# A row maximum that skips NaNs: one load in one piece, no trial write-backs, and a bias given as a number

## The chip, the cores and the metric

The kernel runs on one core of a Trainium2 chip. The metric is device time in microseconds (us) of one execution, lower is better. Of the core's engines it uses ScalarE (ACT in the profile), POOL (GpSimd), VectorE (DVE) and SyncE (SP), which issues all transfers. TensorE has no work.

## What is computed

```python
batch, seq, dim = 32, 2048, 2048
x = np.random.randn(batch, seq, dim).astype(np.float32)
mask = np.random.rand(batch, seq, dim) < 0.1
x[mask] = np.nan
...
def reference(x, axis):        # axis = -1
    return np.nanmax(x, axis=axis).astype(np.float32)
```

The input is 65,536 rows of 2,048 f32 values, 536.87 MB; a tenth of the values are NaN. The output is the largest value of each row that is not NaN, 0.26 MB.

## The kernel before

**Tiles.** The rows are cut into 74 tiles, listed by hand in `TILES` (L16). A tile holds up to 7 rows for each of the 128 partitions, 14,336 columns of 4 bytes, and is counted in quarters of a row (`Q`, 512 columns). Each entry of `TILES` has three lists: how the tile is loaded, in how many pieces it is cleaned, and in how many it is reduced. Most tiles are `[28], [7, 9, 12], [16, 12]`: one load of 28 quarters (7,168 KB in all), three pieces of 7, 9 and 12 quarters, and two reductions of 16 and 12 quarters (4 rows and 3). The first tile is one row, and the last dozen tiles have ever smaller loads and pieces. Below, tiles are counted from 0; `number` in the code is one more.

**What is done with a tile.** A NaN would spoil a maximum, so it is replaced first, by way of the upper 16 bits of each value, read as int16 (every second int16 of the tile):

- ScalarE's *key pass* (L432) reads these halves with a stride of two and writes a dense uint16 key into one of three key buffers `kts`. It computes `Prelu(EDGE - half)`. Its slope `alpha` sends the halves of NaNs, which lie above `EDGE`, to keys that come back as very negative numbers. Its bias `EDGE` (32639.25) is read from memory: `top`, a column of the tile `scalars`, filled at L274.
- The *write-back* turns the key into a half again (`TOP - key`) and writes it into the tile, with a stride of two. POOL does it (L453), or ScalarE for the pieces with a negative sign in `TILES` (L407).
- VectorE's reduction (L478) takes the maximum of the whole f32 rows into `acc`.

At the end of groups of tiles, rows in which nothing was found are marked (`find`, L250) and results are stored (L511).

**What sets the order.** Each engine runs its instructions in the order of the program. `Order` (L119) adds the semaphore waits that data and buffers ask for. Three facts matter for the change:

- There are three tile buffers (`xts`, `BUFS`), so the load of tile n waits until the reductions of tile n - 3 are done (`free`, L346 and L490). SyncE issues loads in order, so a load that waits holds back all behind it.
- A key pass waits for its tile's load, and for a key buffer that the write-backs have left.
- Each load has one of 14 semaphores in turn (`LANES`, L331).

**The parts that the change touches.** `spare` (L280) is called once, after tile 0 (L491). It runs eighteen instructions on columns 2,048 and up of buffer 0, which tile 0 does not use: six on each of POOL, ScalarE and VectorE, in that order, each computing `1 - x` on 1,024 int16 values a partition, with dense, strided and blocked patterns of reading and writing. Their results are read by nothing. What they read is filled with zeros first (L277). The load of tile 3, the next in that buffer, waits for the last of each engine (L492). With `number == SPLIT` (L353) tile 29 is loaded by nine transfers in place of one: for each of four column ranges of 1,024 to 1,408 columns, one transfer for the first 8, 120, 64 or 16 partitions and one for the others (`BLOCKS`), and one for the remaining 9,472 columns.

Of the kernel before, what the change touches and what calls it, by code (L numbers as in the profile page):

```python
# [8 lines left out]
D = 2048  # L9
# [54 lines left out]

LANES = 14

LEFT = D
SOME = 1024
SPLIT = 30
BLOCKS = ((1024, 8), (1152, 120), (1280, 64), (1408, 16))  # L70

# [4 lines left out]
EDGE = TOP + 0.25  # L78
# [99 lines left out]
def kernel(  # L178
# [15 lines left out]
    nc = tc.nc  # L194
    P = nc.NUM_PARTITIONS
    f32, i32 = mybir.dt.float32, mybir.dt.int32
    i16, u16 = mybir.dt.int16, mybir.dt.uint16
    ALU = mybir.AluOpType
    ACT = mybir.ActivationFunctionType
# [7 lines left out]
    of = out.bitcast(i32).flatten_outer_dims().rearrange("r c -> (r c)")  # L207
# [16 lines left out]
    with tc.tile_critical():  # L224
        order = Order(nc)

        def act(deps, pair=None, **kw):
            return order.add(
                "act",
                nc.scalar,  # L230
                lambda: nc.scalar.activation(**kw),  # L231
                deps,
                lane=pair,
                joint=pair is not None,
            )
# [38 lines left out]
        e_top = order.add("dve", nc.vector, lambda: nc.vector.memset(top, EDGE), [])  # L274
        act([e_top], out=warm, in_=top, func=ACT.Prelu, alpha=0.5)

        zeros = xts[0][:, LEFT : LEFT + SOME // 2 + SOME]  # L277
        e_zero = order.add("dve", nc.vector, lambda: nc.vector.memset(zeros, 0), [])  # L278

        def spare(room):  # L280

            half = SOME // 2
            of = room[:, 0:half].bitcast(i16)
            apart = room[:, half : half + SOME].bitcast(i16)[:, 1::2]
            e = e_zero
            ends = []
            at = half + SOME

            def place():
                nonlocal at  # L290
                at += SOME
                return room[:, at - SOME : at].bitcast(i16)

            def turns(v, j):
                return v.rearrange("p (j i) -> p i j", j=j)

            for who, engine in (("pool", nc.gpsimd), ("act", nc.scalar), ("dve", nc.vector)):
                to = place()
                far, near = to[:, 1::2], to[:, 0:SOME]
                forms = [(far, of), (near, of), (near, apart), (far, apart)]  # L300
                forms += [(turns(far, j), turns(of, j)) for j in (2, 32)]
                d = [e]
                for o, i in forms:
                    if who == "act":
                        d = [act(d, out=o, in_=i, func=ACT.Copy, bias=1.0, scale=-1.0)]
                        continue
                    d = [
                        order.add(
                            who,
                            engine,  # L310
                            lambda: engine.tensor_scalar(  # L311
                                out=o, in0=i, scalar1=-1.0, scalar2=1.0, op0=ALU.mult, op1=ALU.add
                            ),
                            d,
                        )
                    ]
                ends += d
            return ends

        free = [[] for _ in range(BUFS)]  # L320
        kfree = [[] for _ in range(NKEYS)]
        clock = 0
# [14 lines left out]
        for gi, (s, g) in enumerate(zip(rows, GROUPS)):  # L337
# [6 lines left out]
            for loads, pieces, reds in g:  # L344
# [4 lines left out]
                at = 0  # L349
                for c in loads:  # L350
                    c *= Q
                    runs = [(at, at + c, 0, P)]
                    if number == SPLIT:  # L353
                        runs = []
                        a = at
                        for n, p in BLOCKS:
                            runs += [(a, a + n, 0, p), (a, a + n, p, P)]
                            a += n
                        runs += [(a, at + c, 0, P)]
                    for a, b, p, q in runs:  # L360
                        e = order.add(
                            "sp",
                            nc.sync,
                            lambda: nc.sync.dma_start(  # L364
                                out=xt[p:q, a:b], in_=xg[p:q, base + a : base + b]
                            ),
                            before + lanes[turn],
                            lane=f"load{turn}",
                            step=16,
                        )  # L370
                        lanes[turn] = [e]
                        turn = (turn + 1) % LANES
                        landed.append((a, b, e))
                    at += c
                clean = []
                after = []
# [42 lines left out]
                for parts in pieces:  # L419
                    parts = parts if isinstance(parts, tuple) else (parts,)  # L420
                    c = int(sum(map(abs, parts))) * Q
                    here = [l for a, b, l in landed if a < at + c and b > at]
                    kold = []
                    if used + c > KEYS:
                        key = (key + 1) % NKEYS
                        used = 0
                        kold, kfree[key] = last(kfree[key]), []
                        assert all(k != key for q in half.values() for _, _, k, _, _ in q)
                        if at + c == sum(loads) * Q:

                            kold = kold + last(kfree[(key + 1) % NKEYS])
                    e_key = act(  # L432
                        here + kold,
                        out=kts[key][:, used : used + c],
                        in_=xt[:, at : at + c].bitcast(i16)[:, 1::2],
                        func=ACT.Prelu,
                        bias=top,
                        scale=-1.0,
                        alpha=float(TOP - LOW) / (EDGE - NAN),
                    )  # L440
                    release()
                    for c in parts:
                        back, wait, c = c < 0, isinstance(c, float), int(abs(c)) * Q
                        kp = kts[key][:, used : used + c]
                        used += c
                        to = xt[:, at : at + c].bitcast(i16)[:, 1::2]
                        at += c
                        if back:
                            held.append((at - c, at, key, kp, e_key, piece))
                            if not wait or at == sum(loads) * Q:  # L450
                                release()
                        else:
                            e = pool(  # L453
                                [e_key],
                                name(piece),
                                out=to,
                                in0=kp,
                                scalar1=-1.0,
                                scalar2=float(TOP),
                                op0=ALU.mult,  # L460
                                op1=ALU.add,
                            )
                            cleaned(at - c, at, key, piece, e)
                        piece += 1
                        open_ = [h[0] for h in held] + [p[0] for q in half.values() for p in q]
                        while reds and done + reds[0] <= min([at] + open_):
                            n = reds.pop(0)


                            lo = done - 1 if done % D else done  # L470
                            done += n
                            row = (base + lo) // D
                            if done % D:
                                m, to = 1, xt[:, done - 1 : done].bitcast(f32)
                            else:
                                m = max(n // D, 1)
                                to = acc[:, row : row + m]
                            e = dve(  # L478
                                [e for a, b, e in clean if b > lo and a < done] + part,
                                nc.vector.tensor_reduce,  # L480
                                out=to,
                                in_=xt[:, lo:done]
                                .bitcast(f32)
                                .rearrange("p (c d) -> p c d", c=m),
                                axis=mybir.AxisListType.X,
                                op=ALU.max,
                            )
                            part = [e] if done % D else []
                            after.append(e)
                free[(number - 1) % BUFS] = after[-1:]  # L490
                if number == 1:  # L491
                    free[0] = free[0] + spare(xt[:, LEFT:])  # L492
                base += at
            stores.append((og, acc.bitcast(i32)))
            if gi == LATE:
# [61 lines left out]
```

## Time and profile before

| what | value |
| --- | --- |
| time, median of 3 runs (lowest to highest) | 1265.29 us (1263.24 to 1266.24) |
| span of the profiled execution | 1263.2 us |
| instructions in the profile | 926 |
| VectorE busy | 1134.3 us (90%), of it reductions 1109.3 |
| ScalarE busy | 1000.7 us (79%), of it key passes 935.1 (247) |
| POOL busy | 1188.0 us (94%), of it write-backs 1171.5 (236) |
| trial write-backs | VectorE 22.2, POOL 15.5, ScalarE 14.4 us (6 each) |
| transfers | 537.2 MB, 425 GB/s over the span |

The profiled execution is one of its own. Its time is the span, from the first instruction to the last; the lowest of the runs lies 0.04 us above it, the median 2.1 us.

In the profile's rows a line number such as L231 can be that of a helper: all ScalarE instructions carry L231, POOL's write-backs L241, VectorE's reductions L248, the trials of POOL and VectorE L311. They are told apart by what they read and write: `kt<-xt,scalars` is a key pass, `xt<-kt` a write-back, `xt<-xt` a trial, `acc<-xt` a reduction. Buffer numbers are left out. A row in order of time has start, length, engine, line, operation, shape of the first instruction merged into it, their count, and in brackets how long the engine had been idle and what ended that. A row of the list of groups has the count, total busy time and mean length in ns, then idle time. A row of the table of waits has the total in us, how often, and the longest. All loads together are the page's DMA row; an engine that moves a part of a transfer counts as busy while it has a packet in flight.

### The profile page before, as it was taken

What the parts mean: (1) busy time and instruction counts of PE and PEld (TensorE: products, weight loads), DVE (VectorE), ACT (ScalarE), POOL (GpSimd) and SP (SyncE); (2) the same over time, 40 slices, a digit from 0 to 9 for tenths busy, and PEclk for the clock granted to TensorE, in tenths of its full rate; (3) what the DMA queues carried; (4) which work ended last, traced back from release to release, by engine and by line L of the source; (5) the groups of instructions that cost most, each with busy time, mean ns of one, the idle gap of its engine ahead of it and who ended that gap; (6) DMA issues with size and microseconds to landing.
All of it is one profiled execution on the core that took longest, in us unless ns stands there. A gap on an engine that the chain in (4) does not pass through costs nothing.

```text
span 1263.2 us, 926 instructions
## 1 busy us (share of the span) xinstructions
DVE 1134.3 (90%) x188; ACT 1000.7 (79%) x279; POOL 1188.0 (94%) x248
## 2 busy tenths in 40 slices
DVE  7788988888889988788888889888888999999999
ACT  7767787778787876678777977777778778999998
POOL 7999989998999899798999899999999999989998
DMA  9999999999999999999999999999999999999997
GB/s 411 407 434 421 436 432 431 436 434 432 434 436 434 436 436 318 439 434 436 434 436 432 432 436 430 434 430 432 434 436 434 436 432 423 432 435 431 427 429 289
DMA packets 16613, 537.20 MB, mean 425 GB/s; under 512 B 2654, under 2 KB 2654, under 8 KB 4190
## 3 DMA queue, kind: packets, MB, share of 16 engines
q1 hardware_dynamic: 16606, 537.14, 99.3%
q14 instruction: 7, 0.06, 0.0%
HBM read 536.87 MB, written 0.26 MB: 425 GB/s over the span
## 4 chain that ended last, share of the span: by engine, by line
DMA 34%; DVE 26%; POOL 25%; ACT 14%; issue 1%; SPq 0%; ACTq 0%
DMA xt<-in_x_dram 34%; DVE acc L248 26%; POOL xt L241 23%; ACT kt L231 13%; ACT xt L231 2%; POOL xt L311 1%; SPq L364 0%; DVE none L254 0%; DVE acc L268 0%; SPq L552 0%; ACTq L163 0%; SPq L224 0%
## 5 line engine op out<-in xcount | busy, mean ns | idle before, releaser
L241 POOL TENSOR_SCALAR xt<-kt 128x3584 int16<-128x3584 uint16 (+11 forms) x236 | 1171.5, 4964 | 69.8 <-ACT kt L231 51.9
L248 DVE TENSOR_REDUCE acc<-xt 128x3 f32<-128x6144 f32 (+4 forms) x175 | 1107.6, 6379 | 124.6 <-POOL xt L241 116.7
L231 ACT ACTIVATE kt<-xt,scalars 128x3584 uint16<-128x3584 int16 (+9 forms) x247 | 935.1, 3825 | 255.2 <-DMA xt<-in_x_dram 223.4
L231 ACT ACTIVATE xt<-kt 128x512 int16<-128x512 uint16 (+6 forms) x24 | 52.8, 2202 | 0.7
L311 DVE TENSOR_SCALAR xt<-xt 128x1024 int16<-128x1024 int16 x6 | 22.2, 3702 | 0.2
L311 POOL TENSOR_SCALAR xt<-xt 128x1024 int16<-128x1024 int16 x6 | 15.5, 2576 | 0.5
L231 ACT ACTIVATE xt<-xt 128x1024 int16<-128x1024 int16 x6 | 14.4, 2402 | 0.2
L231 ACT ACT_TABLE_LOAD x1 | 1.3, 1283 | 0.9 <-SPq L224 0.9
L248 DVE TENSOR_REDUCE xt<-xt 128x1 f32<-128x1536 f32 x1 | 1.7, 1745 | 0.0
L278 DVE MEMSET xt<- 128x1536 int32 x1 | 1.3, 1338 | 0.3 <-issue 0.3
L274 DVE MEMSET scalars<- 128x1 f32 x1 | 0.1, 59 | 1.0 <-SPq L224 1.0
L254 DVE TENSOR_SCALAR none<-acc 128x414 int32<-128x414 f32 (+1 forms) x2 | 0.8, 381 | 0.1
L268 DVE TENSOR_TENSOR acc<-acc,none 128x414 int32<-128x414 int32 (+1 forms) x2 | 0.7, 374 | 0.1
L254 POOL TENSOR_SCALAR late<-acc 128x91 int32<-128x91 f32 x1 | 0.5, 547 | 0.1
L268 POOL TENSOR_TENSOR acc<-acc,late 128x91 int32<-128x91 int32 x1 | 0.3, 341 | 0.1
L538 POOL MEMSET const-float32-0.0<- 128x1 f32 x1 | 0.1, 98 | 0.2 <-issue 0.2
L231 ACT ACTIVATE scalars<-scalars 128x1 f32<-128x1 f32 x1 | 0.2, 203 | 0.0
L538 POOL MEMSET const-bfloat16-1.0<- 128x1 bf16 x1 | 0.1, 102 | 0.0
L538 POOL MEMSET const-uint8-127<- 128x1 uint8 x1 | 0.1, 101 | 0.0
L538 POOL MEMSET const-float32-1.0<- 128x1 f32 x1 | 0.1, 98 | 0.0
## 6 DMA issues: line engine op xcount, KB each, us to landing
xt<-in_x_dram SPq DMA_DIRECT2D x60, 7168.0 KB, 22.5
xt<-in_x_dram SPq DMA_DIRECT2D x2, 5120.0 KB, 17.4
xt<-in_x_dram SPq DMA_DIRECT2D x3, 2816.0 KB, 21.9
xt<-in_x_dram SPq DMA_DIRECT2D x4, 2048.0 KB, 26.9
xt<-in_x_dram SPq DMA_DIRECT2D x5, 1536.0 KB, 28.9
xt<-in_x_dram SPq DMA_DIRECT2D x2, 3584.0 KB, 24.7
xt<-in_x_dram SPq DMA_DIRECT2D x6, 1024.0 KB, 26.0
xt<-in_x_dram SPq DMA_DIRECT2D x3, 1792.0 KB, 30.2
```

Of the source, the lines that this page charges most:

```text
L231: lambda: nc.scalar.activation(**kw),
L241: lambda: nc.gpsimd.tensor_scalar(**kw),
L248: return order.add("dve", nc.vector, lambda: do(**kw), deps)
L254: lambda: engine.tensor_scalar(out=none, in0=acc, scalar1=NONE, scalar2=float(0x00800000), op0=ALU.is_equal, op1=ALU.mult,),
L268: lambda: engine.tensor_tensor(out=bits, in0=bits, in1=none, op=op),
L274: e_top = order.add("dve", nc.vector, lambda: nc.vector.memset(top, EDGE), [])
L278: e_zero = order.add("dve", nc.vector, lambda: nc.vector.memset(zeros, 0), [])
L311: lambda: engine.tensor_scalar(out=o, in0=i, scalar1=-1.0, scalar2=1.0, op0=ALU.mult, op1=ALU.add),
L538: nc = _bacc.Bacc("TRN2", target_bir_lowering=False, num_devices=1)
```

## The change

The function `spare`, its call, the zeros that it reads and its constants go. The load of tile 3 then waits for the reduction of tile 0 alone. Tile 29 is loaded by one transfer, as its neighbours are; the eight transfers fewer shift the turn of the 14 semaphores for all later loads by eight places. The key pass has `bias=EDGE`, a number in the instruction, in place of `top`. `top` itself stays, since one small instruction at the start reads it.

```diff
-LEFT = D
-SOME = 1024
-SPLIT = 30
-BLOCKS = ((1024, 8), (1152, 120), (1280, 64), (1408, 16))
...
-        zeros = xts[0][:, LEFT : LEFT + SOME // 2 + SOME]
-        e_zero = order.add("dve", nc.vector, lambda: nc.vector.memset(zeros, 0), [])
-
-        def spare(room):
-
-            half = SOME // 2
-            of = room[:, 0:half].bitcast(i16)
-            apart = room[:, half : half + SOME].bitcast(i16)[:, 1::2]
...
-            for who, engine in (("pool", nc.gpsimd), ("act", nc.scalar), ("dve", nc.vector)):
-                to = place()
-                far, near = to[:, 1::2], to[:, 0:SOME]
-                forms = [(far, of), (near, of), (near, apart), (far, apart)]
-                forms += [(turns(far, j), turns(of, j)) for j in (2, 32)]
-                d = [e]
-                for o, i in forms:
-                    if who == "act":
-                        d = [act(d, out=o, in_=i, func=ACT.Copy, bias=1.0, scale=-1.0)]
-                        continue
...
-                ends += d
-            return ends
...
-                    runs = [(at, at + c, 0, P)]
-                    if number == SPLIT:
-                        runs = []
-                        a = at
-                        for n, p in BLOCKS:
-                            runs += [(a, a + n, 0, p), (a, a + n, p, P)]
-                            a += n
-                        runs += [(a, at + c, 0, P)]
-                    for a, b, p, q in runs:
-                        e = order.add(
...
-                                out=xt[p:q, a:b], in_=xg[p:q, base + a : base + b]
...
+                    a, b = at, at + c
+                    e = order.add(
+                        "sp",
+                        nc.sync,
+                        lambda: nc.sync.dma_start(
+                            out=xt[:, a:b], in_=xg[:, base + a : base + b]
+                        ),
+                        before + lanes[turn],
...
                         func=ACT.Prelu,
-                        bias=top,
+                        bias=EDGE,
                         scale=-1.0,
...
                 free[(number - 1) % BUFS] = after[-1:]
-                if number == 1:
-                    free[0] = free[0] + spare(xt[:, LEFT:])
```

More of the change, by code (lines that the diff above doesn't have):

```diff
@@ L275 @@
         act([e_top], out=warm, in_=top, func=ACT.Prelu, alpha=0.5)
-        zeros = xts[0][:, LEFT : LEFT + SOME // 2 + SOME]
-        e_zero = order.add("dve", nc.vector, lambda: nc.vector.memset(zeros, 0), [])
-        def spare(room):
-            half = SOME // 2
-            of = room[:, 0:half].bitcast(i16)
-            apart = room[:, half : half + SOME].bitcast(i16)[:, 1::2]
[L285 to L295, printed above, removed]
-            for who, engine in (("pool", nc.gpsimd), ("act", nc.scalar), ("dve", nc.vector)):
-                to = place()
-                far, near = to[:, 1::2], to[:, 0:SOME]
-                forms = [(far, of), (near, of), (near, apart), (far, apart)]
-                forms += [(turns(far, j), turns(of, j)) for j in (2, 32)]
-                d = [e]
-                for o, i in forms:
-                    if who == "act":
-                        d = [act(d, out=o, in_=i, func=ACT.Copy, bias=1.0, scale=-1.0)]
-                        continue
[L307 to L316, printed above, removed]
-                ends += d
-            return ends
         free = [[] for _ in range(BUFS)]
@@ L351 @@
                     c *= Q
-                    runs = [(at, at + c, 0, P)]
-                    if number == SPLIT:
-                        runs = []
-                        a = at
-                        for n, p in BLOCKS:
-                            runs += [(a, a + n, 0, p), (a, a + n, p, P)]
-                            a += n
-                        runs += [(a, at + c, 0, P)]
-                    for a, b, p, q in runs:
-                        e = order.add(
-                            "sp",
-                            nc.sync,
-                            lambda: nc.sync.dma_start(
-                                out=xt[p:q, a:b], in_=xg[p:q, base + a : base + b]
[L366 to L373, printed above, removed]
+                    a, b = at, at + c
[6 more added lines that the diff above has]
+                        before + lanes[turn],
+                        lane=f"load{turn}",
+                        step=16,
+                    )
+                    lanes[turn] = [e]
+                    turn = (turn + 1) % LANES
+                    landed.append((a, b, e))
                     at += c
```

## The prediction

> **What bounds the kernel now.** I read the page's slices first, for the transfer rate along the span: each slice is 31.6 us.
>
> ```profile
> DMA  9999999999999999999999999999999999999997
> GB/s 411 407 434 421 436 432 431 436 434 432 434 436 434 436 436 318 439 434 436 434 436 432 432 436 430 434 430 432 434 436 434 436 432 423 432 435 431 427 429 289
> ```
>
> The 16 engines have work throughout and move some 434 GB/s, except in the first four slices, in one at 474 to 505 us (318) and in the last. Next the table of waits, ScalarE's and SyncE's, and ScalarE's rows in order of time. A row that ends in "DMA" begins when a tile's load has landed.
>
> ```profile
> ACT kt L231 <- DMA xt<-in_x_dram: 223.4, 61, 7.4
> ...
> SPq L163 <- DVE xt L311: 32.8, 1, 32.8
> ```
>
> ```profile
> 22.77 7.31 ACT L231 ACTIVATE kt<-xt,scalars 128x3584 uint16<-128x3584 int16 x2 [0.38 <-DMA xt<-in_x_dram]
> ...
> 75.22 7.31 ACT L231 ACTIVATE kt<-xt,scalars 128x3584 uint16<-128x3584 int16 x2 [1.28 <-DMA xt<-in_x_dram]
> ...
> 92.09 7.31 ACT L231 ACTIVATE kt<-xt,scalars 128x3584 uint16<-128x3584 int16 x2 [1.30 <-DMA xt<-in_x_dram]
> ...
> 111.50 7.31 ACT L231 ACTIVATE kt<-xt,scalars 128x3584 uint16<-128x3584 int16 x2 [3.88 <-DMA xt<-in_x_dram]
> ...
> 145.40 9.44 ACT L231 ACTIVATE kt<-xt,scalars 128x4608 uint16<-128x4608 int16 x2 [3.89 <-DMA xt<-in_x_dram]
> ```
>
> ```profile
> 466.69 7.31 ACT L231 ACTIVATE kt<-xt,scalars 128x3584 uint16<-128x3584 int16 x2 [3.96 <-DMA xt<-in_x_dram]
> ...
> 485.55 7.31 ACT L231 ACTIVATE kt<-xt,scalars 128x3584 uint16<-128x3584 int16 x2 [5.85 <-DMA xt<-in_x_dram]
> ...
> 508.59 9.44 ACT L231 ACTIVATE kt<-xt,scalars 128x4608 uint16<-128x4608 int16 x2 [6.86 <-DMA xt<-in_x_dram]
> 525.41 7.31 ACT L231 ACTIVATE kt<-xt,scalars 128x3584 uint16<-128x3584 int16 x2 [7.38 <-DMA xt<-in_x_dram]
> ```
>
> Counting tiles from 0, tile 8 lands at 145.40 and tile 27 at 466.69: 321.29 / 19 = 16.91 us a tile. That is the undisturbed pace of the loads. The engines fit under it: POOL needs 4.20 + 5.34 + 7.04 and three gaps of 0.08, 16.82 us; VectorE 15.15; ScalarE 12.7. So up to about 1046 us the loads set the time. From there it is VectorE:
>
> ```profile
> 1046.50:1260.50 214.00, 213.37 (x59) 200.23 (x85) 199.53 (x64) 1.00 0.97 414
> ```
>
> The columns are the stretch, its length, then busy time of VectorE, ScalarE and POOL. VectorE rests 0.6 us in 214, so the end comes 214 us after tile 60's reductions may start, and that is set by landings.
>
> **The split load** (tile 29, nine transfers in place of one). From tile 27 (466.69) to tile 30 (525.41) are 58.72 us; three undisturbed tiles take 3 x 16.91 = 50.73. The nine cost **8.0 us**, which the slice at 318 GB/s confirms: 31.6 x (435 - 318) / 435 = 8.5. ScalarE waits 5.85, 6.86 and 7.38 us for these tiles, so no engine had work in hand to cover the delay, and by tile 31 (542.31, 16.90 later) the old pace is back; nothing later regains it. I take all 8.0. Eight issues leave SyncE's queue too, which is not busy.
>
> **The eighteen trial write-backs** (six on each engine, L311 and L231). ScalarE's end at 22.39 and POOL's at 26.42; both lie in the wait for tile 1 (22.77, and 3.4 us more for POOL), so they hide but for some 0.3 us on POOL. VectorE's last from 12.71 to 35.09. They delay no reduction, but POOL's real write-backs of tile 1 run beside them. POOL's rows of this stretch, then of an undisturbed one (300 to 330 us):
>
> ```profile
> L241 POOL TENSOR_SCALAR xt<-kt 128x4608 int16<-128x4608 uint16 x1 | 7.4, 7428 | 0.1
> ...
> L241 POOL TENSOR_SCALAR xt<-kt 128x3584 int16<-128x3584 uint16 x1 | 6.3, 6252 | 0.1
> ```
>
> ```profile
> L241 POOL TENSOR_SCALAR xt<-kt 128x4608 int16<-128x4608 uint16 x2 | 10.7, 5338 | 0.2
> L241 POOL TENSOR_SCALAR xt<-kt 128x3584 int16<-128x3584 uint16 x2 | 8.4, 4197 | 3.7 <-ACT kt L231 3.6
> ```
>
> That is 2.09 + 2.05 = 4.14 us, and with the start 0.3 late POOL is 4.4 behind. At 16.82 against 16.91 it cannot win this back by itself; so tile 1's reductions begin at 40.29 and end at 55.44, its buffer is reloaded late, and the loads slip instead. Load 4, issued at 55.44, lands 75.22 - 39.70 - 2 x 16.91 = 1.7 us late; load 6 lands 111.50 - 92.09 - 16.91 = 2.5 late, though issued 3.0 us ahead of load 5's landing. Checked over the whole start: tile 8 stands at 145.40; undisturbed it would be 22.77 + 7 x 16.91 = 141.14. Loss **4.26 us**.
>
> Without the trials the pace should hold from tile 1. In the undisturbed chain from a landing to the last reduction are 28.18 us (229.90 to 258.08 in the chain of waits); tile 1 would end at 22.77 + 28.2 = 50.95, 5.6 us ahead of tile 3's landing at 56.6, and the same 5.6 follows for each tile after. Load 3, which now waits for all trials (SyncE's 32.8 us above, issue at 35.1), would wait for the first reduction alone and go out at 12.8; it queues behind loads 1 and 2 until 39.70, so it lands when it did. What is queued behind it on SyncE (load 4) waits for 50.95 anyway. Bounds for this term: 1.7 (only the first slip goes) to 4.3. I take 4.25. The memset of `zeros` (1.34 us) lies before the first landing at 5.91 and is worth nothing.
>
> **The bias as a number** (247 key passes). In the instruction list of the changed program they read `xt` alone, no longer `scalars`. The price is bounded by two rows, the first a trial that reads with a stride and writes densely as the key pass does, with a number as bias:
>
> ```profile
> L231 ACT ACTIVATE xt<-xt 128x1024 int16<-128x1024 int16 x1 | 1.1, 1057 | 0.0
> ```
>
> ```profile
> L231 ACT ACTIVATE kt<-xt,scalars 128x1024 uint16<-128x1024 int16 x7 | 7.7, 1130 | 0.0
> ```
>
> So 73 ns less for each. Unrelated key passes overlap by 0.09 us now (7.31 for 3.28 + 4.12); if that overlap went with the memory operand, the net would be 0.02 worse. I take 0.07 better. Up to 1046 us it buys nothing, since ScalarE waits 223 us for loads; if that cover went, 181 x 0.073 = 13 us would count. From 1046 it has VectorE's unbroken work as cover. What is left is the start of that work: two key passes ahead of the last waits of VectorE (0.37 and 0.53 us), 0.1 us.
>
> **Sum.** 8.0 + 4.25 + 0.1 = 12.35 us off the span of 1263.2: 1250.85. The shown runs have a median of 1265.29, 2.1 above that span, so the forecast is 1265.29 - 12.35 = **1252.9 us**.
>
> **Rivals.** (a) *Only the split's time comes back.* POOL's margin is 0.09 us a tile, and a load issued 3.0 us ahead slipped once (load 6) and once did not (load 5, issued at 72.25); if some other early delay puts the loads on that edge, the start is lost again: 1265.3 - 8.0 = 1257.3. Against it: the 4.14 us have their cause in VectorE's trials, and five of the tiles of the first part give POOL 4.2 us of rest.
>
> (b) *VectorE takes back the 8.0:* its pause at the split would have been rest it needs. 1265.3 - 4.35 = 1261. Against: it waits 1.7 us before each tile ahead of the split.
>
> (c) *ScalarE's saving reaches the end.* The chain of waits runs through ScalarE from 1219.89 to 1239. With 66 key passes after 1050 us, 66 x 0.073 = 4.8: 1248.1. Against: VectorE's 213.37 of 214. The Trainium skill, "ScalarE: Activation LUTs", section "What ACT_TABLE_LOAD costs", says that a pointer operand adds about 93 ns; this trace's pair gives 73, and with 93 this rival would stand at 1246.8 (an estimate from that page).
>
> (d) *Slower: a key pass with a number runs at the write-backs' pace.* ScalarE's other instructions with a number, the write-backs, take 4195 ns for 3584 elements and 776 for 512, 1.113 ns each; the key pass 5413 for 6144 and 705 for 512, 0.836. After 1050 us ScalarE passes 186,368 elements: x 0.277 = 51.6 us more, less 66 x 0.07, less its 13.8 us of rest: 33 us, giving 1286. It decides the end from 0.935 ns an element on, and cancels the gain at 1.00. Against: the 1057 ns row; the write-backs write with a stride.
>
> **How the numbers follow.** Forecast 0.72, (a) 0.12, (b) 0.05, (c) 0.05, (d) 0.04, and 0.02 for no change. The forecast's own range is 1250.3 to 1255.4: the runs of before spread by 3.0 us, and the start term can lose up to 2.5. With (a), and part of (c), the range is 1249 to 1258. About 0.2% (2.5 us) is what a measurement can tell from no change; faster holds the forecast, (a), (b) and (c): 0.93, same 0.02, slower 0.05.
>
> **What would show it.** Key passes that wait on a landing every 16.9 us from 22.77 on, tile 27 near 462.4, tile 30 near 513.2; POOL's two write-backs of tile 1 at 4.2 and 5.3 us; no slice at 318; key passes of 1024 at about 1.06 us; VectorE unbroken for 214 us before the end. A late landing before 120 us would speak for (a), VectorE busy without rest before 1030 for (b), rests of VectorE near the end for (c), key passes of 3584 above 3.3 us for (d).

## The result and the profile after

| | median of runs | span of the profiled execution |
| --- | --- | --- |
| before | 1264.26 us (1261.58 to 1266.24, 4 runs) | 1263.2 us |
| after | 1252.84 us (1252.67 to 1252.94, 4 runs) | 1251.1 us |

The ratio is 0.9911, with a 95% interval of 0.9896 to 0.9925: 11.4 us less by the medians, 12.1 by the two profiled spans. The spread of the runs shrank from 4.7 to 0.3 us.

The slices of the changed kernel's page, its load rate along the span:

```profile
DMA  9999999999999999999999999999999999999997
GB/s 415 440 413 438 440 440 440 411 440 440 440 436 415 440 440 436 436 418 440 440 436 436 418 440 440 436 435 420 440 440 437 431 424 436 428 438 429 428 427 297
```

The slice at 318 GB/s is gone. The values of 411 to 424 that are left come every fifth slice while the landings below keep their step, so I don't read them as stalls. ScalarE's rows in order of time, of the start and around tile 29, each beginning with a landing:

```profile
22.64 7.12 ACT L227 ACTIVATE kt<-xt 128x3584 uint16<-128x3584 int16 x2 [14.96 <-DMA xt<-in_x_dram]
...
73.41 7.12 ACT L227 ACTIVATE kt<-xt 128x3584 uint16<-128x3584 int16 x2 [4.07 <-DMA xt<-in_x_dram]
...
90.28 7.12 ACT L227 ACTIVATE kt<-xt 128x3584 uint16<-128x3584 int16 x2 [4.04 <-DMA xt<-in_x_dram]
...
107.19 7.12 ACT L227 ACTIVATE kt<-xt 128x3584 uint16<-128x3584 int16 x2 [4.08 <-DMA xt<-in_x_dram]
...
141.04 9.26 ACT L227 ACTIVATE kt<-xt 128x4608 uint16<-128x4608 int16 x2 [4.08 <-DMA xt<-in_x_dram]
```

```profile
463.11 7.13 ACT L227 ACTIVATE kt<-xt 128x3584 uint16<-128x3584 int16 x2 [4.06 <-DMA xt<-in_x_dram]
...
513.79 7.12 ACT L227 ACTIVATE kt<-xt 128x3584 uint16<-128x3584 int16 x2 [4.08 <-DMA xt<-in_x_dram]
```

Tiles 4, 5 and 6 now follow each other at 16.87 and 16.91 us. Tile 8 lands at 141.04 (145.40 before), and tiles 27 to 30 take 50.68 us (58.72 before). POOL's first two write-backs of tile 1, from the groups of 23 to 42 us:

```profile
L237 POOL TENSOR_SCALAR xt<-kt 128x4608 int16<-128x4608 uint16 x1 | 5.3, 5317 | 0.1
L237 POOL TENSOR_SCALAR xt<-kt 128x3584 int16<-128x3584 uint16 x1 | 4.2, 4175 | 15.7 <-ACT kt L227 15.7
```

They are at their undisturbed length (7428 and 6252 ns before). The last stage, by busy time of VectorE, ScalarE and POOL:

```profile
1034.49:1248.50 214.01, 213.35 (x59) 195.25 (x85) 199.45 (x63) 1.00 0.97 417
```

It is as long as before and as full on VectorE, and begins 12.06 us earlier, by VectorE's rows before and after:

```profile
1046.55 23.80 DVE L248 TENSOR_REDUCE acc<-xt 128x4 f32<-128x8192 f32 x4 [0.53 <-POOL xt L241]
```

```profile
1034.49 23.80 DVE L244 TENSOR_REDUCE acc<-xt 128x4 f32<-128x8192 f32 x4 [0.51 <-POOL xt L237]
```

The gain, then, was made almost wholly in the landings, 11.6 us of it by tile 30 (525.41 to 513.79), and VectorE's closing run was moved, not shortened.

### The profile page after: what moved, and what is told of

Read it like the earlier page. It is cut to its first block, busy times and chain, and to the rows that moved or that the text cites. A ratio compares the mean times of both kernels' runs of the same rounds, so it can differ in the third digit from the quotient of the medians.

```text
span 1251.1 us, 893 instructions
## 1 busy us (share of the span) xinstructions
DVE 1110.8 (89%) x181; ACT 965.6 (77%) x273; POOL 1168.4 (93%) x242
## 4 chain that ended last, share of the span: by engine, by line
DMA 40%; DVE 29%; POOL 22%; ACT 9%; issue 1%; SPq 0%
DMA xt<-in_x_dram 40%; DVE acc L244 29%; POOL xt L237 22%; ACT kt L227 8%; ACT xt L227 1%; SPq L309 0%; DVE none L250 0%; DVE acc L264 0%; SPq L495 0%; SPq L220 0%
## 5 line engine op out<-in xcount | busy, mean ns | idle before, releaser
L227 ACT ACTIVATE kt<-xt 128x3584 uint16<-128x3584 int16 (+9 forms) x247 | 913.4, 3734 | 278.2 <-DMA xt<-in_x_dram 258.1
## 6 DMA issues: line engine op xcount, KB each, us to landing
xt<-in_x_dram SPq DMA_DIRECT2D x4, 2048.0 KB, 22.3
```

## The experiments

All times below are medians. The experiments were run in three groups, each with the kernel before beside it: the first four below (it had 1264.85 us), then VectorE's six alone, POOL's and ScalarE's twelve, the late issue and the eight small loads (1264.91), then the other four (1265.76). Only the ratio to it has an interval; differences between two experiments rest on the spreads of their runs, and across groups also on these medians, which lie 0.9 us apart and 0.6 to 1.5 above the one in the table.

### Each part alone

The first three take one part of the change each, the fourth all but the bias.

**One load for tile 29.**

```diff
-                    if number == SPLIT:
+                    if number == -SPLIT:
```

> The kernel before with tile 29 in one load, trials and bias in memory kept. My theory (the parts add up): 8.0 us less than before, tile 8 still lands near 145.4 us, tile 30 lands near 517.4 instead of 525.4. Rival (b), VectorE needs the pause: under 4 us less, VectorE without rests after 500 us.

Measured: 1256.79 us (1256.15 to 1257.10), ratio 0.9935 (0.9922 to 0.9949): 8.06 less. Its landings:

```profile
144.72 4.14 ACT L231 ACTIVATE kt<-xt,scalars 128x4608 uint16<-128x4608 int16 x1 [3.43 <-DMA xt<-in_x_dram]
```

```profile
466.72 7.31 ACT L231 ACTIVATE kt<-xt,scalars 128x3584 uint16<-128x3584 int16 x2 [3.86 <-DMA xt<-in_x_dram]
...
517.43 7.31 ACT L231 ACTIVATE kt<-xt,scalars 128x3584 uint16<-128x3584 int16 x2 [3.89 <-DMA xt<-in_x_dram]
```

Tile 8 is still late (144.72, after 145.40 in the profile before and 141.04 in the changed kernel) and tile 30 stands where it was expected. Rival (b) falls: VectorE gives nothing back.

**No trials.**

```diff
-        zeros = xts[0][:, LEFT : LEFT + SOME // 2 + SOME]
-        e_zero = order.add("dve", nc.vector, lambda: nc.vector.memset(zeros, 0), [])
+        e_zero = None
...
-                if number == 1:
-                    free[0] = free[0] + spare(xt[:, LEFT:])
```

> The kernel before without the eighteen trials, split and bias in memory kept. My theory: 4.25 us less than before, tile 8 lands near 141.1, POOL's write-backs of tile 1 take 4.2 and 5.3 us, the split still costs 8.0 between tiles 27 and 30. Rival (a), the start slips anyway: within 1 us of before, a late landing before 120 us.

Measured: 1259.88 us (1259.54 to 1260.01), ratio 0.9962 (0.9949 to 0.9974): 4.97 less. Its landings of tiles 8, 27 and 30:

```profile
141.17 9.44 ACT L231 ACTIVATE kt<-xt,scalars 128x4608 uint16<-128x4608 int16 x2 [3.88 <-DMA xt<-in_x_dram]
```

```profile
463.17 7.31 ACT L231 ACTIVATE kt<-xt,scalars 128x3584 uint16<-128x3584 int16 x2 [3.85 <-DMA xt<-in_x_dram]
...
520.82 7.31 ACT L231 ACTIVATE kt<-xt,scalars 128x3584 uint16<-128x3584 int16 x2 [7.37 <-DMA xt<-in_x_dram]
```

Rival (a) falls: the start does not slip. The split costs 57.65 - 50.68 = 7.0 us here, where 8.0 was expected: one less than behind the late start of the profile before.

**The bias as a number, alone.**

```diff
-                        bias=top,
+                        bias=EDGE,
```

> The kernel before with the key pass's bias as a number, the only change (the column in memory stays filled). My theory: 0 to 0.2 us less than before, key passes about 0.07 to 0.09 us shorter, the end still set by VectorE. Rival (c), ScalarE's saving reaches the end: 4 us less or more.

Measured: 1263.97 us (1261.53 to 1266.17), ratio 0.9994 (0.9985 to 1.0003). No change can be told, within a spread of 4.6 us, but 4 us is excluded. In its profile, with trials and split, tile 8 lands at 144.71 and tiles 27 to 30 take 526.41 - 466.83 = 59.58 us: the split costs 8.9 us there.

**All but the bias.** The changed kernel with `bias=top`.

> The changed kernel with the key pass's bias in memory again, the only difference to it. My theory: 0.1 us slower than the changed kernel, so about 1253.0 us. Rival (c): 4 us slower, 1257. A third reading, that the shorter key pass keeps the loads ahead of their edge: landings slip somewhere before 1030 us and the time is 1 to 3 us longer.

Measured: 1253.18 us (1253.07 to 1253.18), 0.34 above the changed kernel, whose runs end at 1252.94. The two were run beside different runs of before, so I read this as some tenths of a microsecond at most. The profiles give the share of the bias: from tile 60's landing to VectorE's closing run are 1046.55 - 1033.21 = 13.34 us before, 1034.76 - 1021.41 = 13.35 here, and 1034.49 - 1021.34 = 13.15 in the changed kernel, 0.2 us less. Its last stage, and its key passes of 1,024 beside those of the changed kernel:

```profile
1034.80:1248.90 214.10, 213.38 (x59) 200.31 (x85) 199.84 (x63) 1.00 0.97 414
```

```profile
L227 ACT ACTIVATE kt<-xt,scalars 128x1024 uint16<-128x1024 int16 x7 | 7.7, 1129 | 0.0
```

```profile
L227 ACT ACTIVATE kt<-xt 128x1024 uint16<-128x1024 int16 x7 | 7.1, 1039 | 0.0
```

The number takes 0.09 us off each key pass, and 200.31 - 195.25 = 5.1 us off ScalarE in the last stage, whose length stays at 214. Rival (c) falls, and for the reason given: VectorE has 213.4 us of work there either way.

### Which trials cost

The next five are the changed kernel with some of `spare` put back (the loop over engines cut to the names given), or with its wait alone.

**VectorE's six alone.**

```diff
-            for who, engine in (("pool", nc.gpsimd), ("act", nc.scalar), ("dve", nc.vector)):
+            for who, engine in (("dve", nc.vector),):
```

> The changed kernel with VectorE's six trials and their zeros put back (load 3 waits for them again). My theory: VectorE's trials alone slow POOL's first two write-backs of tile 1 to about 6.2 and 7.4 us, and nearly all of the start's loss comes back: tile 8 lands near 145, time about 1257. Rival: it was the chain of all three engines; then no slip, 1252.9.

Measured: 1253.15 us (1252.98 to 1253.28). My theory failed. VectorE's trials in the kernel before, then here, with POOL's first write-backs of tile 1, in order of time:

```profile
12.71 22.38 DVE L311 TENSOR_SCALAR xt<-xt 128x1024 int16<-128x1024 int16 x6
```

```profile
12.52 7.97 DVE L311 TENSOR_SCALAR xt<-xt 128x1024 int16<-128x1024 int16 x6
...
26.00 16.70 POOL L241 TENSOR_SCALAR xt<-kt 128x3584 int16<-128x3584 uint16 x3 [15.72 <-ACT kt L231]
```

Alone they take 7.97 us, not 22.38, and end before tile 1 has landed.

**POOL's and ScalarE's twelve** (the loop over `pool` and `act`).

> The changed kernel with POOL's and ScalarE's twelve trials put back, none on VectorE. My theory: they hide in the wait for tile 1 but for 0.3 us; POOL's write-backs of tile 1 take 4.2 and 5.3 us, tile 8 lands near 141.1, time within 0.5 us of 1252.9. Rival (POOL's late start is not won back and the loads slip): 1254 or more.

Measured: 1252.95 us (1252.93 to 1253.10). They hide, as expected.

**The late issue of load 3, without trials.**

```diff
                 free[(number - 1) % BUFS] = after[-1:]
+                if number == 2:
+                    free[0] = free[0] + [clean[1][2]]
```

> The changed kernel in which load 3 waits also for POOL's second write-back of tile 1, so that it is issued near 35.4 us as before, not at 12.6; no trials. My theory: the late issue costs nothing, 1252.9, tile 8 near 141.1. Rival (the start's loss came from the late issue of load 3): tile 4 or 6 lands late and the time is 1255 to 1257.

Measured: 1253.15 us (1253.00 to 1253.32). SyncE's 32.8 us of waiting, its longest single wait before, cost next to nothing, but not quite nothing: load 3 goes out at 35.52, and tile 3 lands 56.93 - 39.56 = 17.37 us after tile 2, half a microsecond late, which tile 8 still shows (141.57, where 141.1 was expected).

```profile
56.93 7.12 ACT L227 ACTIVATE kt<-xt 128x3584 uint16<-128x3584 int16 x2 [4.55 <-DMA xt<-in_x_dram]
```

The rival's 1255 to 1257 is excluded.

**POOL's and VectorE's twelve** (the loop over `pool` and `dve`), run after the three above.

> The changed kernel with POOL's and VectorE's twelve trials put back, none on ScalarE. VectorE's trials alone took 8.0 us, with all three engines' 22.4. Theory as it now stands (POOL's and VectorE's trials hold each other up, so VectorE's run on beside the real write-backs): VectorE's trials again about 22 us, the first two write-backs of tile 1 at 6.2 and 7.4 us, time about 1256 to 1257. Rival (ScalarE's are needed too): VectorE's trials end before 26 us, 1253.

Measured: 1255.53 us (1255.33 to 1256.45), 2.7 above the changed kernel, and tile 27 lands 2.9 later than there (465.98 against 463.11). The same two engines in order of time, then POOL's groups of 23 to 50 us:

```profile
10.40 15.76 POOL L311 TENSOR_SCALAR xt<-xt 128x1024 int16<-128x1024 int16 x6
12.55 22.28 DVE L311 TENSOR_SCALAR xt<-xt 128x1024 int16<-128x1024 int16 x6
...
26.24 54.50 POOL L241 TENSOR_SCALAR xt<-kt 128x3584 int16<-128x3584 uint16 x9
```

```profile
L241 POOL TENSOR_SCALAR xt<-kt 128x4608 int16<-128x4608 uint16 x1 | 7.4, 7442 | 0.1
```

VectorE's trials are back at 22 us, the second write-back at 7.4, and POOL runs on without rest, as in the profile before. ScalarE's trials are not needed for it.

**VectorE's six, held back to run beside POOL's write-backs.** `spare` is called in tile 1, behind its first key pass, and waits for that pass.

```diff
-                d = [e]
+                d = [e, after_key]
...
+                    if number == 2 and at == 0:
+                        free[0] = free[0] + spare(xts[0][:, LEFT:], e_key)
```

> The changed kernel with VectorE's six trials alone, held back until ScalarE's first key pass of tile 1, so that they run beside POOL's write-backs of tile 1 and no trial of POOL's is there. If running beside VectorE's trials is what slows a write-back: the first two take over 5 and 6 us, POOL falls behind by 2 us or more and the loads slip by 1 to 4 us, 1254 to 1257. Rival (the slow write-backs were an after-effect of POOL's own trials): 4.2 and 5.3 us, 1253.

Measured: 1274.10 us (1274.07 to 1274.28), ratio 1.0066 (1.0054 to 1.0079), slower than before and far from both figures:

```profile
25.97 32.12 DVE L311 TENSOR_SCALAR xt<-xt 128x1024 int16<-128x1024 int16 x6 [13.32 <-ACT kt L231]
26.02 38.97 POOL L241 TENSOR_SCALAR xt<-kt 128x3584 int16<-128x3584 uint16 x6 [15.69 <-ACT kt L231]
...
39.64 7.12 ACT L231 ACTIVATE kt<-xt 128x3584 uint16<-128x3584 int16 x2 [3.54 <-DMA xt<-in_x_dram]
...
58.12 15.01 SPq L364 DMA_DIRECT2D xt<-in_x_dram  x2
```

Beside the real write-backs VectorE's six take 32.12 us, four times their 7.97. The write-backs lengthen too: POOL's six take 38.97, where twice the 16.70 above is usual. This is not as expected in its parts. The first two write-backs take 4.73 and 5.37 us, not over 5 and 6 (4.18 and 5.32 beside no trial), and those beside VectorE's last two trials, the blocked ones, take 7.39 and 9.15 (5.33 and 7.04 otherwise). Taken one by one, the records look as if each instruction waited out the other's. VectorE's fifth trial runs from 44.28 to 50.58 and ends 2.3 us after a write-back that ends at 48.28; the write-back begun at 48.36 is 2.06 longer than usual. In the kernel before it is the same two trials that reach tile 1's first two write-backs, which are 2.05 and 2.09 longer: the 4.14 us of the prediction.

But the time is set by another thing: load 3 waits for the trials, is issued at 58.12, and the loads before it had all landed at 39.6. The 16 transfer engines ran dry for some 20 us (1274.1 - 1252.8 = 21.3), so the time says nothing of the slowed write-backs.

### What in the split costs

Three forms of nine transfers for tile 29, in the changed kernel (built from the kernel before, without the call of `spare` and with the bias as a number). The fourth pair of the original is 16 and 112 partitions, the third 64 and 64, the first two 8 and 120.

**Eight small loads over all 128 partitions.**

```diff
-                            runs += [(a, a + n, 0, p), (a, a + n, p, P)]
+                            runs += [(a, a + n // 2, 0, P), (a + n // 2, a + n, 0, P)]
```

> The changed kernel (no trials, bias as a number) with tile 29 in nine loads again, but each over all 128 partitions: eight of 512 to 704 columns and the one of 9,472. Number of transfers is as before, their shape even. If the count of transfers costs the 8.0 us: 1260.9. If it is the uneven partitions (8, 120, 16, 112): about 1253 to 1254, tiles 27 to 30 in 50.8 to 52 us. I expect the second, since each neighbour's issue takes some 0.4 us and the queue holds 17 us of work.

**Four pairs of 64 and 64.**

```diff
-                            runs += [(a, a + n, 0, p), (a, a + n, p, P)]
+                            runs += [(a, a + n, 0, P // 2), (a, a + n, P // 2, P)]
```

> The changed kernel (no trials, bias as a number) with tile 29 in nine loads: four pairs, each of the partitions 0 to 63 and 64 to 127, and the one of 9,472 columns. If only unequal parts cost time: as with nine loads over all partitions, about 1253.4. If any part that does not cover all 128 partitions costs, because rows then go through other engines than usual: 1.5 to 2 us a pair, 1259 to 1261.

**Four pairs of 8 and 120.**

```diff
-BLOCKS = ((1024, 8), (1152, 120), (1280, 64), (1408, 16))
+BLOCKS = ((1024, 8), (1152, 8), (1280, 8), (1408, 8))
```

> The changed kernel with tile 29 in nine loads: four pairs, each of the first 8 partitions and the other 120, and the one of 9,472 columns. If unequal parts cost most: more than the 6.7 us that the mixed split costs beside a start without slips (1259.9 against 1253.2), so 1261 to 1265. If each pair costs the same whatever its parts: 1259.5.

Measured, with the time from tile 27's landing to tile 30's:

| nine transfers | time | tiles 27 to 30 |
| --- | --- | --- |
| none (the changed kernel) | 1252.84 us | 50.68 us |
| all 128 partitions | 1253.37 us | 514.25 - 463.23 = 51.02 |
| pairs of 64 and 64 | 1259.09 us | 519.65 - 462.94 = 56.71 |
| pairs of 8 and 120 | 1260.37 us | 521.07 - 463.02 = 58.05 |

Those of the halves, from ScalarE's rows:

```profile
462.94 7.12 ACT L231 ACTIVATE kt<-xt 128x3584 uint16<-128x3584 int16 x2 [4.07 <-DMA xt<-in_x_dram]
...
519.65 7.12 ACT L231 ACTIVATE kt<-xt 128x3584 uint16<-128x3584 int16 x2 [7.57 <-DMA xt<-in_x_dram]
```

Eight transfers more cost next to nothing when each covers all partitions. Equal halves cost 6.0 us, 1.5 a pair, and the uneven pairs 7.4, 1.8 a pair: that a load covers a part of the partitions is most of the price, how uneven the parts are the smaller rest. The original's three uneven pairs and one even come to 3 x 1.84 + 1.51 = 7.0 by these, as measured without trials. The windows of 5 us of the kernel with halves show the rate meanwhile (last column):

```profile
475.00:480.00 5.00, 4.15 (x1) 0.75 (x1) 4.92 (x2) 1.00 0.78 277
480.00:485.00 5.00, 5.00 (x2) 3.84 (x2) 3.50 (x2) 1.00 1.02 247
485.00:490.00 5.00, 5.00 (x1) 4.62 (x2) 4.92 (x2) 1.00 1.24 297
```

The transfer engines are busy (0.78 to 1.24, next to last column; 1.01 in the mean, since a packet counts whole in the window in which it starts), yet move 250 to 300 GB/s: their packets take longer. The trace's packet records show it directly. A packet of 4,096 bytes to half the partitions takes 270 ns in the median, two of 2,048 bytes to all partitions 2 x 84; one of 5,632 takes 395, two of 2,816 take 2 x 112. Summed over the 16 engines these packets take 10.4 us in place of 6.3, which is 4.1 of the 6.0. The neighbouring tile's load loses with them (tile 28 lands 18.22 us after tile 27). Why packets to a part of the partitions are slower was not tried and stays open. No version faster than the changed kernel came out of this.

## Why the prediction was right, point by point

**The bound.** Right: landings up to VectorE's closing run, then 214 us of it. Both traces have it, and the kernel with the bias in memory again, which gives ScalarE 5 us more work there without a longer stage.

**The split, 8.0 us.** Right: 8.04 between the profiles (58.72 - 50.68), 8.06 by itself. It is 7.0 beside a clean start (6.7 by the times, 1259.88 - 1253.18), so the two parts overlap by a microsecond or a little more. The overlap lies in the split, which cost 8.0 and 8.9 us in the two profiles with a late start and 7.0 in the one without; why was not tried.

**The trials, 4.25 us.** Right in the landings of the start (tile 8 at 141.04, forecast 141.14) and right that a slowed POOL, not the late issue of load 3, makes the loads slip. One step of the working was wrong: that POOL's trials "hide but for some 0.3 us on POOL" and that VectorE's trials are the cause by themselves. VectorE's alone cost nothing (1253.15), POOL's with ScalarE's nothing (1252.95), POOL's with VectorE's 2.7. POOL's trials hide themselves, but stretch VectorE's from 8.0 to 22.3 us, and only so do VectorE's reach the real write-backs. I had read their 22.4 us as their own length. The term was also somewhat too large. The clean start was not fully kept: tile 27 lands at 463.11, not 462.4, by two slips described below, so that by then the trials are worth 466.69 - 463.11 = 3.6 us. The times agree: 1256.79 - 1253.18 = 3.6 beside the missing split (4.97 beside the split, where the overlap counts).

**The bias, 0.1 us.** Right in size for the end: the path from tile 60's landing to VectorE's closing run is 0.2 us shorter with the number; the rest of the 0.34 measured is not the bias as far as the profiles show. The term of 73 ns for each key pass was too small: 1130 to 1039 is 91 ns, and the overlap of key passes remains (3.19 + 4.03 - 7.12 = 0.10), so it is a net gain. The Trainium skill's 93 ns for a pointer operand ("ScalarE: Activation LUTs", section "What ACT_TABLE_LOAD costs") agrees with that.

**The sum.** 12.35 forecast; 12.1 between the profiled spans. By the landings of the two profiles the trials give 3.6, the split 8.0, small slips between tiles 30 and 60 another 0.25 (a lead of 11.62 us grows to 1033.21 - 1021.34 = 11.87), and the bias 0.2. The trials' term was 0.7 us too large, and slips that the prediction did not have made up for a part of it. The 2.1 us between span and median that the forecast adds back are no oddity of that profile but the usual distance between a run's time and its span: the changed kernel's profiled run took 1252.88 us with a span of 1251.1, and runs of the kernel before with a span of 1263.2 took 1265.1 to 1265.2. The forecast time of 1252.9 was worked from a median of 1265.29 over three runs of a kernel that spreads by 4.7 us; with more runs of before its median is 1264.3 to 1265.8. That the time fell on 1252.84 to a tenth is luck within this spread; that the split and the late start are the two costs is not.

**Rival (d)** fell with the key pass of 3,584 at 3.19 us, where 3.3 was the mark.

## What to carry to other kernels

Where transfers set the pace, read the landings: the interval between them in an undisturbed stretch, times the number of tiles, tells to about a microsecond what a disturbance costs. How long the issuing queue waits matters little; how far ahead of the previous landing the next load goes out does. At the usual 5.6 us here the pace held. At 4.0 (load 3 of the late issue) it lost half a microsecond, at 3.0 and 1.1 (loads 6 and 4 before) 2.5 and 1.7, though load 5 at 2.9 lost nothing, and a load issued 18.5 us after the landing cost 21. Keep loads over all 128 partitions; in this kernel count did little, cutting partitions much. Before a long instruction is blamed for slowing another engine, ask what it would last alone: here the length itself came from the other engine.

## What the runs showed of the hardware

- **VectorE and POOL hold each other up** in these int16 operations: VectorE's six took 7.97 us alone, 22.3 beside POOL's trials, 32.1 beside POOL's write-backs, and POOL's write-backs of 4,608 went from 5.3 to 7.4 us. The starts and ends read as if one waited for the other's instruction; no run tested that. The reductions show nothing of it: four rows take 8.69 us beside write-backs, and 8.67 in the one stretch where POOL rests (72.7 us, with VectorE's trials held back).
- **Instruction fetches seem to shift the loads, where nothing else has.** In the changed kernel the trace has packets of 8,192 bytes on the instruction queue at 246.3, 254.5, 385.8 and 940.1 us, and the landings of tiles 15, 23 and 56, due just after, come 17.50, 17.37 and 17.24 us after the tile ahead; the others up to tile 61 come after 16.87 to 16.97. A fetch at 999.1 moved no landing. The shift is not won back in the rest of the run. With POOL's and ScalarE's trials the fetches are at 212.4, 221.0, 379.3 and 906.2, and tiles 13, 23 and 54 are the late ones. But in the kernel before the fetches at 216.7, 224.3, 331.5 and 893.3 moved no landing (the one at 977.3 may have: tile 57 comes 17.57 us after tile 56), and with POOL's and VectorE's trials none of those at 223.3, 250.5, 330.9, 944.3 and 967.8 did. There the transfer engines had already drifted apart: the 16 completions of tile 8's load spread over 2.6 and 2.0 us, against 0.3 in the changed kernel. A fetch on an engine that is ahead would then delay nothing, which is a reading. No run removed a fetch.
- **The spread of the runs tends to shrink with the disturbances:** 4.7, 4.0, 3.8 and 1.3 us with trials and split (the kernel before beside each group), 1.0 with trials alone, 0.5 with the split alone, 0.3 with neither. The 1.3, over nine runs, shows that this is no rule.
